# Rows of u of 1152 bytes instead of 1032, and buffers that begin at multiples of 128 bytes

## Chip, cores and metric

One Trainium2 chip; the kernel runs on one of its cores. The metric is the device time of one execution in microseconds (us), the median of several runs.

## What is computed

One decoder layer on 256 tokens of width 1024 in float32: a SwiGLU block (FFN), a mixer (a state-space branch and a retention branch side by side, gated and merged), a second FFN, and a last norm. Each of the three blocks reads `u`, the normed and modulated residual stream:

```python
u = modulate(rms_norm(h, norm_ffn1_w[l]), sh1, sc1)
h = h + FFN_RESIDUAL_WEIGHT * g1[:, None, :] * swiglu(u, ffn1_w_in[l], ffn1_w_out[l])
u = modulate(rms_norm(h, norm_mix_w[l]), sh2, sc2)
h = h + g2[:, None, :] * hybrid_mixer(u, positions, mix_w_in[l], ...)
u = modulate(rms_norm(h, norm_ffn2_w[l]), sh3, sc3)
h = h + FFN_RESIDUAL_WEIGHT * g3[:, None, :] * swiglu(u, ffn2_w_in[l], ffn2_w_out[l])
return rms_norm(h, norm_final_w)
```

In the FFNs `u` (256x1024) is multiplied by 1024x5632 and the result by 2816x1024; in the mixer `u` is multiplied by 1024x13344, and three smaller products follow.

## The kernel before

**Layout.** Features lie on the 128 partitions and tokens along the free dimension, so `u` is 8 rows (`kt`, 128 features each) of 256 tokens in every partition. Every large product is made of float32r matmuls in three terms: each operand is split into a high part and a remainder (`uh`/`ul`, `ah`/`al`, `wh`/`wl`), and `mm3` (lines 135 to 137) issues high·high, high·remainder and remainder·high into the same PSUM bank.

**Weights.** `load` brings 1 MB of weights into one of four stage buffers `wst` (8192 bytes per partition) through SyncE's DMA queue (line 111). `half` makes 512 KB of it into `wh` (a ScalarE copy, line 126) and `wl` (a VectorE subtraction, line 127), each of four buffers of 4096 bytes. TensorE then runs the matmuls of that half.

**Which operand moves.** A matmul has a stationary operand (loaded as weights of the array, 128 columns here) and a moving one, which streams through it (256, 258 or 512 columns here).
- `pair_project` and the first stage: weight halves stationary, a row of `uh` or `ul` moves, 256 columns. 48 matmuls for a 1 MB load.
- `early_project` runs the first four column blocks of a block on `u` that is not yet normed, with two more columns that hold the shift: 258 columns (`wide_at`). This is why a row of `u` has `T + 2` = 258 elements, 1032 bytes.
- `contract` and the branch steps (`bs`, `br`): weight halves stationary, rows of `ah`/`al` or of the mixer's slots (named `s`) move, 256 columns.
- `v_tile` (the `v` steps): slices of `u` stationary, weight halves move, 512 columns. The last contraction: `ah`/`al` stationary, weight halves move, 512 columns in its first block and 256 in the other two.

**The order of the work** is written out: loops in the FFNs, the table `ORDER` in the mixer. Each engine runs its instructions in that order and waits on semaphores. Other weights (for the modulation, `ada_w`) pass through the same stage buffers and are reduced on VectorE (line 179).

**Where a tile lies.** Pools stack their tiles one behind another in each partition, each at the next multiple of 32 bytes. In this program `wst`, `wh` and `wl` begin at 96 beyond a multiple of 128; `uh` too, `ul` at 32. A row of 1032 bytes moves the start by 8 bytes from row to row. The pools `fp` and `mx`, which hold `ah`, `al` and the slots, begin at a multiple of 128, with rows of 1024 bytes.

**The step scale of the state-space branch.** `dt_tile` computes a softplus on 64 columns in small tiles (`both`, `dtv`, ...). `decays` sends its result through DRAM (`rows`), and GpSimd's queue (POOL) loads it back as masks in buffers of the tag `m` (`wide`, five buffers) in the steps `ml.0` to `ml.3`.

Of the kernel before, what the change touches and what calls it, by code (L numbers as in the profile page):

```python
# [12 lines left out]
F32 = mybir.dt.float32  # L13
F32R = mybir.dt.float32r
# [4 lines left out]
P = 128  # L19
T = 256  # L20
D = 1024
KD = D // P
# [3 lines left out]
NH = 32  # L26
# [8 lines left out]
V_GB, V_SN, V_RN = 216, 232, 248  # L35
V_DS, V_DTB, V_AL = 264, 280, 312
N_VEC = 344

K_ID, K_TRI, K_M = 0, 128, 256
K_INV, K_SGN = 384, 385  # L40
# [37 lines left out]
def layer(ctx: ExitStack, tc: tile.TileContext, a, out, packing):  # L78
# [3 lines left out]
    cst = ctx.enter_context(tc.tile_pool(name="cst", bufs=1))  # L82
    wp = ctx.enter_context(tc.tile_pool(name="wp", bufs=1))
    sp = ctx.enter_context(tc.tile_pool(name="sp", bufs=1))
# [6 lines left out]
    def nm(s):  # L91
        uid[0] += 1
        return f"{s}_{uid[0]}"
# [36 lines left out]
    def split_into(hi, lo, src):  # L130
        act.copy(hi, src)
        dve.tensor_tensor(lo, src, hi.bitcast(F32), ALU.subtract)
# [17 lines left out]
    mean_m = k[:, K_M:K_M + P]  # L150
    ones = cst.tile([P, P], F32, name="ones")
    dve.memset(ones, 1.0)
    epsc = cst.tile([P, 1], F32, name="epsc")
    dve.memset(epsc, EPS)

    phase = {"load": None, "uses": []}
# [9 lines left out]
        with tc.issue_after(phase["load"]):  # L166
            phase["uses"].append(act.activation(*args, **kw).ins)

    col = cst.tile([P, N_VEC], F32, name="col")
    cb = cst.tile([P, D], F32, name="cb")  # L170
    raw = cst.tile([P, N_MOD, KD], F32, name="raw")
    modc = cst.tile([P, N_MOD, KD], F32, name="modc")
# [39 lines left out]
        return rs  # L212

    def new_u():
        full = [sp.tile([P, KD, T + 2], F32R, tag=n, name=nm(n), bufs=1) for n in ("uh", "ul")]
        return tuple(t[:, :, :T] for t in full) + tuple(full)

    def u_tile(u, f, t, jsh):
        sh = modc[:, jsh, f:f + 1]
        act.activation(u[0][:, f, :], t, AF.Identity, bias=sh)  # L220
        dve.scalar_tensor_tensor(u[1][:, f, :], t, sh, u[0][:, f, :].bitcast(F32),
                                 ALU.add, ALU.subtract)
# [20 lines left out]
    def modulated(ha, u, jsh, w, cols):  # L243
        rs = []
        ps = early_project(w, cols, u, 1, lambda: rs.append(rstd(sums, mean_m)))
        rs = rs[0]
        for f in range(KD):
            t = ha(f)
            dve.tensor_tensor(t, t, rs, ALU.mult)
            u_tile(u, f, t, jsh)  # L250
        b = sp.tile([P, 4], F32, tag="eb", name=nm("eb"), bufs=1)
        for i in range(4):
            dve.tensor_copy(b[:, i:i + 1], ps[i][:, T:T + 1])
            dve.tensor_tensor(ps[i][:, :T], ps[i][:, :T], rs, ALU.mult)
        return [(ps[i][:, :T], b[:, i:i + 1]) for i in range(4)]

    def early_project(w, cols, u, at_kt, between):
        sts = [load(w, 0, KD, c0, 256) for c0 in cols]
        ps = [proj_ps().rearrange("p f t -> p (f t)") for _ in range(2)]
        ps += [misc_ps() for _ in range(2)]  # L260
        for kh in range(2):
            hv = [half(st[:, 4 * kh:4 * kh + 4, :]) for st in sts]
            for kk in range(4):
                kt = 4 * kh + kk
                if kt == at_kt:
                    between()
                for i in range(2):
                    for f in range(2):
                        mm3(ps[2 * i + f][:, :T + 2], at(hv[i], al, kk, slice(f * P, (f + 1) * P)),
                            wide_at(u, kt), kt == 0, kt == KD - 1)  # L270
        return ps
# [63 lines left out]
    with tc.tile_pool(name="ep", bufs=1) as ep:  # L335
# [4 lines left out]
        for i in range(2):  # L340
            fetch(h[:, 4 * i:4 * i + 4, :].rearrange("p f t -> p (f t)"), "x",
                  lambda m, i=i: m[:, 512 * i:512 * i + 512].T.reshape(4, P, T).transpose(1, 0, 2))
# [133 lines left out]
    with tc.tile_pool(name="mx", bufs=1, reuse_waits="tile") as mx:  # L476
# [6 lines left out]
        def small(shape, tag, bufs=1):  # L483
            return mx.tile(shape, F32, tag=tag, name=nm(tag), bufs=bufs)

        def wide(shape, dt=F32):
            return mx.tile(shape, dt, tag="m", name=nm("m"), bufs=WIDE_BUFS)
# [2 lines left out]
        bT, cT = slot([P, 4, T]), slot([P, 4, T])  # L490

        dskip = col[:, V_DS:V_DS + 16]
        dtb, ahead = col[:, V_DTB:V_DTB + NH], small([P, NH], "ahead")
        rows = dp.tile([2, NH, P], F32, name="rows")

        def conv_pair(f0, dst):
# [17 lines left out]
        def need(t):  # L514
            if now[0] != t:
                now[0] = t
                table(table_of[t])
# [4 lines left out]
        def dt_tile():  # L522
            need("e")
            st = load(w_in, 0, KD, C_DT, NH)
            wd = wp.tile([P, 1024], F32R, tag="wh", name=nm("wh"), bufs=HALF_BUFS)
            wd = wd[:, :KD * 2 * NH].rearrange("p (k n) -> p k n", k=KD)
            split_into(wd[:, :, :NH], wd[:, :, NH:], st)
            ps = proj_ps()
            for kt in range(KD):
                uh, ul = at(u, al, kt)  # L530
                if kt:
                    pe.matmul(ps[:NH, 0, :], wd[:, kt, :NH], ul, start=False, stop=False)
                pe.matmul(ps[:2 * NH, 0, :], wd[:, kt, :], uh, start=kt == 0, stop=kt == KD - 1)
                if not kt:
                    pe.matmul(ps[:NH, 0, :], wd[:, kt, :NH], ul, start=False, stop=False)
            both = small([2 * NH, NH], "both")
            dve.tensor_tensor(both, ident[:2 * NH, :NH], ident[:2 * NH, NH:2 * NH], ALU.add)
            dtr = wide([2 * NH, T])
            act.copy(dtr, ps[:2 * NH, 0, :])
            ps = misc_ps()  # L540
            for c in range(2):
                pe.matmul(ps[:, c * NH:(c + 1) * NH], dtr[:, c * P:(c + 1) * P], both,
                          start=True, stop=True)
            v, e, s1, s2, pl = (small([P, 2, NH], n) for n in ("dtv", "dte_", "dts", "dts2", "dtp"))
            dve.tensor_tensor(v, ps[:, :64].rearrange("p (c h) -> p c h", c=2),
                              dtb.unsqueeze(1).broadcast_to([P] + x2), ALU.add)
            act.activation(e, v, AF.Abs)
            lookup(ahead, col[:, V_AL:V_AL + NH], AF.Exp)
            lookup(e, e, AF.Exp, scale=-1.0)
            dve.tensor_scalar(s1, e, 2.0, None, ALU.add)  # L550
            dve.reciprocal(s1, s1)
            dve.tensor_tensor(s1, s1, e, ALU.mult)
            dve.tensor_tensor(s2, s1, s1, ALU.mult)
            dve.tensor_scalar(pl, s2, 1.0 / 17, None, ALU.mult)
            for n in (15, 13, 11, 9, 7, 5, 3):
                dve.scalar_tensor_tensor(pl, pl, 1.0 / n, s2, ALU.add, ALU.mult)
            dve.scalar_tensor_tensor(pl, pl, 1.0, s1, ALU.add, ALU.mult)
            dve.tensor_scalar(v, v, 0.0, None, ALU.max)
            dve.scalar_tensor_tensor(dt, pl, 2.0, v, ALU.mult, ALU.add)
            dve.scalar_tensor_tensor(av, dt, -1.0, ahead.unsqueeze(1).broadcast_to([P] + x2),  # L560
                                     ALU.mult, ALU.mult)
# [310 lines left out]
        for q in range(2):  # L872
            for p2 in range(2):
                r = slice(2 * p2, 2 * p2 + 2)
                t = tot_r[q][:, r, :]
# [9 lines left out]
        def ha(f):  # L885
            return hA[f // 4][:, f % 4, :]
# [4 lines left out]
    with tc.tile_pool(name=nm("fp"), bufs=1, reuse_waits="tile") as fp:  # L891
# [43 lines left out]
        for bi, (c0, n) in enumerate(blocks):  # L935
# [15 lines left out]
            for tt in range(2):  # L951
                t = fp.tile([P, 512], F32, tag="t", name=nm("t"), bufs=2)[:, :n]
# [66 lines left out]
```

## Time and profile before

| | |
|---|---|
| median of 3 runs | 863.01 us (862.42 to 863.12) |
| the profiled execution | 864.84 us |
| its span, first to last instruction | 863.1 us |
| mean granted TensorE clock | 0.995 |
| PE busy | 847.8 us |
| DVE busy | 670.6 us |
| ACT busy | 509.2 us |
| HBM | 190.96 MB read, 223 GB/s over the span |

Matmuls overlap: one lasts about 0.28 us in the profile, but the next starts long before it ends. What a matmul costs is read from start to start, which is called its pace below. The profiled execution is 1.7 us longer than its span, and 1.8 us above the median of the runs without a profile.

### The profile page before, as it was taken

Reading aid. Unit: us, or ns where it says so; the run is one execution under the profiler, and the core shown is the slowest. Engines: PE = TensorE matmul, PEld = TensorE weight load, DVE = VectorE, ACT = ScalarE, POOL = GpSimd, SP = SyncE. Lnnn points to the kernel's source line nnn. Section 1 sums busy time; section 2 is a strip of 40 time slices with the busy share of each in tenths; the row PEclk is TensorE's granted clock in tenths of the full one; section 3 lists DMA queues with packets and bytes.
Section 4 is the critical chain, followed back from the end, with each engine's and each line's share of the span. In section 5 each row is a group of like instructions: output and inputs, shape, how many; then the busy total and the mean of one; then the engine's idle time right before and its main releaser. Section 6 shows DMA issues by size and latency. Waiting matters only on the chain.

```text
span 863.1 us, 16252 instructions
## 1 busy us (share of the span) xinstructions
PE 847.8 (98%) x6752; PEld 822.1 (95%) x6752; DVE 670.6 (78%) x1020; ACT 509.2 (59%) x722; POOL 10.3 (1%) x21
## 2 busy tenths in 40 slices
PE   6999999999999999999999999999999999999996
PEld 5999999999999989899999999999999999999896
DVE  6989798986989887688797778977979975455463
ACT  5355445455888687766464558765558644545342
POOL 0000000000110010000000000000000000000000
PEclk9999999999999999999999999999999999999998
DMA  9968878994595555445557664554554785454521
GB/s 350 414 247 323 312 272 311 359 355 161 189 319 194 191 185 177 177 147 196 196 196 293 222 221 156 211 205 156 218 213 180 260 317 189 154 185 176 189 87 49
DMA packets 30588, 193.09 MB, mean 224 GB/s; under 512 B 3489, under 2 KB 4001, under 8 KB 10802
## 3 DMA queue, kind: packets, MB, share of 16 engines
q1 hardware_dynamic: 28658, 186.34, 59.1%
q0 software_dynamic: 1568, 5.28, 1.9%
q8 instruction: 53, 0.87, 0.4%
q10 hardware_dynamic: 288, 0.44, 0.2%
q14 instruction: 21, 0.17, 0.1%
HBM read 190.96 MB, written 1.08 MB: 223 GB/s over the span
## 4 chain that ended last, share of the span: by engine, by line
PE 88%; issue 4%; DVE 3%; ACT 2%; DMA 2%; SPq 0%; DVEq 0%; ACTq 0%; POOLq 0%
PE proj L137 27%; PE proj L135 27%; PE proj L136 27%; PE misc L135 1%; PE misc L137 1%; PE misc L136 1%; DVE wl L127 1%; DMA ada<-in_ada_w_dram 1%; ACT wh L126 1%; DMA m<-rows 1%; PE misc L686 1%; PE misc L830 1%; PE misc L203 1%; DVE ada L179 0%; PE misc L696 0%
## 5 line engine op out<-in xcount | busy, mean ns | idle before, releaser
L126 ACT CAST wh<-wst 128x1024 fp32r<-128x1024 f32 (+3 forms) x281 | 289.6, 1034 | 265.9 <-PE proj L136 178.8
L127 DVE TENSOR_TENSOR wl<-wst,wh 128x1024 fp32r<-128x1024 f32 (+3 forms) x281 | 336.9, 1202 | 134.5 <-ACT wh L126 133.8
L135 PE MATMUL proj<-uh,wh 128*128 128x256 f32 (+1 forms) x1328 | 373.6, 282 | 2.3 <-ACT uh L220 2.3
L137 PE MATMUL proj<-uh,wl 128*128 128x256 f32 (+1 forms) x1328 | 374.7, 282 | 0.0
L136 PE MATMUL proj<-ul,wh 128*128 128x256 f32 (+1 forms) x1328 | 373.6, 282 | 0.0
L135 PEld LDWEIGHTS proj<-uh,wh 128*128 128x128 f32 x1328 | 250.1, 189 | 2.8 <-ACT uh L220 2.5
L136 PEld LDWEIGHTS proj<-ul,wh 128*128 128x128 f32 x1328 | 251.3, 189 | 0.3 <-issue 0.2
L137 PEld LDWEIGHTS proj<-uh,wl 128*128 128x128 f32 x1328 | 251.4, 189 | 0.2 <-issue 0.2
L135 PE MATMUL proj<-s,wh 128*128 128x256 f32 x320 | 89.9, 282 | 1.1 <-ACT s L752 0.8
L136 PE MATMUL proj<-s,wh 128*128 128x256 f32 x320 | 89.2, 279 | 0.0
L137 PE MATMUL proj<-s,wl 128*128 128x256 f32 x320 | 89.2, 279 | 0.0
L179 DVE SCALAR_TENSOR_TENSOR wst<-wst,cb 128x1024 f32<-128x1024 f32 x56 | 67.3, 1219 | 5.7 <-DMA wst<-in_ada_w_dram 5.6
L135 PEld LDWEIGHTS proj<-s,wh 128*128 128x128 f32 x320 | 60.0, 188 | 2.1 <-ACT s L752 1.7
L136 PEld LDWEIGHTS proj<-s,wh 128*128 128x128 f32 x320 | 60.2, 188 | 0.0
L137 PEld LDWEIGHTS proj<-s,wl 128*128 128x128 f32 x320 | 60.1, 188 | 0.0
L137 PE MATMUL proj<-ah,wl 128*128 128x256 f32 x176 | 49.1, 279 | 0.0
L135 PE MATMUL proj<-ah,wh 128*128 128x256 f32 x176 | 49.1, 279 | 0.0
L136 PE MATMUL proj<-al,wh 128*128 128x256 f32 x176 | 49.1, 279 | 0.0
L136 PE MATMUL proj<-wl,ah 128*128 128x256 f32 (+1 forms) x132 | 42.1, 319 | 0.0
L137 PE MATMUL proj<-wh,al 128*128 128x256 f32 (+1 forms) x132 | 42.1, 319 | 0.0
L135 PE MATMUL proj<-wh,ah 128*128 128x256 f32 (+1 forms) x132 | 42.1, 319 | 0.0
L159 ACT ACT_TABLE_LOAD x30 | 38.5, 1283 | 1.2 <-PEq L992 0.7
(234 smaller groups left out, 1069.0 us busy)
## 6 DMA issues: line engine op xcount, KB each, us to landing
wst<-in_mix_w_in_dram SPq DMA_DIRECT2D x52, 1024.0 KB, 4.9
wst<-in_ffn_w_in_dram SPq DMA_DIRECT2D x37, 1024.0 KB, 5.0
wst<-in_ada_w_dram SPq DMA_DIRECT2D x28, 1024.0 KB, 6.1
wst<-in_ffn_w_out_dram SPq DMA_DIRECT2D x17, 1024.0 KB, 4.9
ada<-in_ada_w_dram SPq DMA_DIRECT2D x16, 512.0 KB, 11.9
wst<-in_w_br_ssd_dram SPq DMA_DIRECT2D x8, 1024.0 KB, 4.9
wst<-in_w_br_ret_dram SPq DMA_DIRECT2D x8, 1024.0 KB, 5.2
wst<-in_ffn_w_in_dram SPq DMA_DIRECT2D x7, 896.0 KB, 12.6
```

Source lines behind the costliest of these rows:

```text
L126: act.copy(hi, v)
L127: dve.tensor_tensor(lo, v, hi.bitcast(F32), ALU.subtract)
L135: pe.matmul(o, l[0], r[0], start=first, stop=False, skip_group_check=skip)
L136: pe.matmul(o, l[0], r[1], start=False, stop=False, skip_group_check=skip)
L137: pe.matmul(o, l[1], r[0], start=False, stop=last, skip_group_check=skip)
L159: ins = act.preload_act_table_set(name).ins
L179: dve.scalar_tensor_tensor(st[:, i, :], st[:, i, :], 1.0, cb, ALU.mult, ALU.mult, accum_out=raw[:, j, f0 + i:f0 + i + 1])
L203: pe.matmul(ps[:, :T], mean, s, start=i == 0, stop=i == len(parts) - 1)
L686: pe.matmul(py[hh * 64:hh * 64 + 64, f * T + c * P:f * T + (c + 1) * P], xd[:, c, hl * 64:hl * 64 + 64], m[c][:, hl, :], start=True, stop= ...
L830: pe.matmul(py[:, eh, :], v[:, 0, es], sc[:, :T], start=True, stop=False)
```

## The change

A row of `u` gets 288 elements (1152 bytes, nine times 128), of which 256 or 258 are used as before. Small tiles ahead of the large ones (`epsc`, `col`) are padded so that the next large tile begins at a multiple of 128 bytes, and the tile `eb` behind them too. The small tiles of `dt_tile` become parts of one tile `work`, which takes a turn of the `m` buffers.

```diff
+LINE = 128
+U_ROW = T + LINE // 4
+PAD = 16
...
-    epsc = cst.tile([P, 1], F32, name="epsc")
+    epsc = cst.tile([P, LINE // 4], F32, name="epsc")[:, :1]
...
-    col = cst.tile([P, N_VEC], F32, name="col")
+    col = cst.tile([P, N_VEC + PAD], F32, name="col")[:, :N_VEC]
...
     def new_u():
-        full = [sp.tile([P, KD, T + 2], F32R, tag=n, name=nm(n), bufs=1) for n in ("uh", "ul")]
-        return tuple(t[:, :, :T] for t in full) + tuple(full)
+        full = [sp.tile([P, KD, U_ROW], F32R, tag=n, name=nm(n), bufs=1) for n in ("uh", "ul")]
+        return tuple(t[:, :, :T] for t in full) + tuple(t[:, :, :T + 2] for t in full)
...
-        b = sp.tile([P, 4], F32, tag="eb", name=nm("eb"), bufs=1)
+        b = sp.tile([P, LINE // 4], F32, tag="eb", name=nm("eb"), bufs=1)
...
-        dtb, ahead = col[:, V_DTB:V_DTB + NH], small([P, NH], "ahead")
+        dtb = col[:, V_DTB:V_DTB + NH]
...
-            both = small([2 * NH, NH], "both")
+            work = wide([P, 12, NH])
+            both, ahead = work[:2 * NH, 10], work[:, 11]
...
-            v, e, s1, s2, pl = (small([P, 2, NH], n) for n in ("dtv", "dte_", "dts", "dts2", "dtp"))
+            v, e, s1, s2, pl = (work[:, 2 * i:2 * i + 2] for i in range(5))
```

Where the tiles begin, in bytes from the start of a partition, as the pools place them (in brackets the remainder by 128):

| tile | before | after |
|---|---|---|
| `wst`, first of 4 | 26720 (96) | 26880 (0) |
| `wh`, first of 4 | 59488 (96) | 59648 (0) |
| `wl`, first of 4 | 75872 (96) | 76032 (0) |
| `uh`, row kt | 92256 + 1032 kt (96, 104, 112, 120, 0, 8, 16, 24) | 92416 + 1152 kt (0) |
| `ul`, row kt | 100512 + 1032 kt (32, 40, 48, 56, 64, 72, 80, 88) | 101632 + 1152 kt (0) |
| `ah`, row f | 117120 + 1024 f (0) | 119296 + 1024 f (0) |
| slots, 4096 bytes each | from 117120 (0) | from 119296 (0) |

No engine's instructions change their number, place or shape. What changes beside addresses is one wait, on GpSimd's queue. These are its rows of the steps `decays` (`rows<-m`) and `ml.0` and `ml.1` (two loads of `m` and two of `ec` each); in brackets the semaphores that a row waits for. Before:

```order
L624 DMA rows<-m_2669 32x2x128 [waits DVE_49]
L656 DMA m_2673<-rows 128x1024 [waits DMASW0_49]
L656 DMA m_2674<-rows 128x1024
L659 DMA ec_2672<-rows 64x4x128 x2
L656 DMA m_2680<-rows 128x1024
L656 DMA m_2681<-rows 128x1024 [waits PE_49,Activation_49]
L659 DMA ec_2679<-rows 64x4x128 x2
```

And now:

```order
L629 DMA rows<-m_2663 32x2x128 [waits DVE_49]
L661 DMA m_2667<-rows 128x1024 [waits DMASW0_49]
L661 DMA m_2668<-rows 128x1024
L664 DMA ec_2666<-rows 64x4x128 x2
L661 DMA m_2674<-rows 128x1024 [waits PE_49,Activation_49]
L661 DMA m_2675<-rows 128x1024 [waits Activation_49]
L664 DMA ec_2673<-rows 64x4x128 x2
```

Nothing moved. `work` takes one turn of the five `m` buffers, so that the first load of `ml.1` gets the buffer that `dtr` had (the wait for PE and ScalarE) and the second the one that `work` had (the added wait for ScalarE); before, the first got a fresh buffer.

## Rows read from the trace of the kernel before

**Rows 1.** The profile's page, its first line and the busy time of each engine (us, share of the span, instructions).

```profile
span 863.1 us, 16252 instructions
...
PE 847.8 (98%) x6752; PEld 822.1 (95%) x6752; DVE 670.6 (78%) x1020; ACT 509.2 (59%) x722; POOL 10.3 (1%) x21
```

**Rows 2.** Who TensorE (PE) waited for over the whole span: us in total, number of waits, the longest. These are the two largest of seven.

```profile
PE misc L360 <- DMA crow<-in_c_dram: 2.4, 1, 2.4
PE proj L135 <- ACT uh L220: 2.3, 1, 2.3
```

**Rows 3.** The page's chain of work that ended last, by engine, as shares of the span.

```profile
PE 88%; issue 4%; DVE 3%; ACT 2%; DMA 2%; SPq 0%; DVEq 0%; ACTq 0%; POOLq 0%
```

**Rows 4.** Timeline of PE, first and last matmul of an unbroken run in which u is the moving operand: 432 matmuls (nine pair projections of 48) in the mixer. Columns: start in us, duration in us, engine, line, operation, output<-inputs, array shape, shape of the moving operand.

```profile
456.58 0.28 PE L135 MATMUL proj<-uh,wh 128*128 128x256 f32 x1
...
507.82 0.28 PE L137 MATMUL proj<-uh,wl 128*128 128x256 f32 x1
```

**Rows 5.** The same, first and last matmul of two unbroken runs in which another tile moves: the 528 matmuls of the first FFN's contraction (`ah` and `al`), and 96 of two branch steps (the slots `s`).

```profile
146.05 0.28 PE L135 MATMUL proj<-ah,wh 128*128 128x256 f32 x1
...
207.54 0.28 PE L137 MATMUL proj<-ah,wl 128*128 128x256 f32 x1
...
422.54 0.28 PE L135 MATMUL proj<-s,wh 128*128 128x256 f32 x1
...
433.63 0.28 PE L137 MATMUL proj<-s,wl 128*128 128x256 f32 x1
```

**Rows 6.** The same for the last contraction, in which the weight halves move and `ah` and `al` are stationary: 132 matmuls of 512 columns, then 264 of 256 columns.

```profile
793.64 0.39 PE L135 MATMUL proj<-wh,ah 128*128 128x512 f32 x1
...
824.20 0.40 PE L137 MATMUL proj<-wh,al 128*128 128x512 f32 x1
824.43 0.28 PE L135 MATMUL proj<-wh,ah 128*128 128x256 f32 x1
...
855.56 0.27 PE L137 MATMUL proj<-wh,al 128*128 128x256 f32 x1
```

**Rows 7.** The same for one v step, in which the weight halves move and slices of u are stationary: 24 matmuls of 512 columns.

```profile
357.93 0.39 PE L135 MATMUL proj<-wh,uh 128*128 128x512 f32 x1
...
363.25 0.39 PE L137 MATMUL proj<-wh,ul 128*128 128x512 f32 x1
```

**Rows 8.** The same in the early projection ahead of the second FFN, 258 columns with u moving: the first and last of 49 matmuls.

```profile
670.07 0.28 PE L136 MATMUL misc<-ul,wh 128*128 128x258 f32 x1
...
675.82 0.28 PE L136 MATMUL misc<-ul,wh 128*128 128x258 f32 x1
```

**Rows 9.** Timeline of PE in the first microseconds of matmuls, two neighbours; then one stretch: us, busy us and instructions (x) of PE, PEld, DVE, ACT and POOL, the granted clock (a share of full speed), the DMA engines' share and GB/s.

```profile
20.71 0.41 PE L136 MATMUL proj<-ul,wh 128*128 128x256 f32 x1
20.92 0.41 PE L137 MATMUL proj<-uh,wl 128*128 128x256 f32 x1
...
19.40:22.00 2.60, 2.60 (x14) 2.60 (x14) 2.60 (x8) 1.73 (x3) 0.00 (x0) 0.50 1.01 411
```

**Rows 10.** Groups of PE instructions by line and shape (L135 alone; L136 and L137 have the same number each): count (x) | busy us, mean ns of one | idle us before.

```profile
L135 PE MATMUL proj<-uh,wh 128*128 128x256 f32 x1296 | 364.2, 282 | 2.3 <-ACT uh L220 2.3
L135 PE MATMUL proj<-s,wh 128*128 128x256 f32 x320 | 89.9, 282 | 1.1 <-ACT s L752 0.8 <-ACT s L131 0.2
...
L135 PE MATMUL proj<-ah,wh 128*128 128x256 f32 x176 | 49.1, 279 | 0.0
...
L135 PE MATMUL proj<-wh,uh 128*128 128x512 f32 x64 | 26.0, 406 | 0.0
...
L135 PE MATMUL proj<-wh,ah 128*128 128x256 f32 x88 | 24.7, 281 | 0.0
...
L135 PE MATMUL proj<-wh,ah 128*128 128x512 f32 x44 | 17.4, 395 | 0.0
...
L135 PE MATMUL misc<-uh,wh 128*128 128x256 f32 x48 | 13.2, 290 | 0.0
...
L135 PE MATMUL proj<-uh,wh 128*128 128x258 f32 x32 | 9.4, 294 | 0.0
```

**Rows 11.** Groups of ScalarE (ACT) and VectorE (DVE) instructions by line and shape, same columns.

```profile
L126 ACT CAST wh<-wst 128x1024 fp32r<-128x1024 f32 x255 | 267.1, 1049 | 248.5 <-PE proj L136 173.3 <-issue 37.4 <-PE proj L137 28.6
...
L131 ACT CAST s<-s 128x1024 fp32r<-128x1024 f32 x4 | 4.2, 1051 | 3.6 <-DVE s L728 3.6
...
L127 DVE TENSOR_TENSOR wl<-wst,wh 128x1024 fp32r<-128x1024 f32 x255 | 310.6, 1221 | 130.0 <-ACT wh L126 129.4 <-PE proj L136 0.2
...
L132 DVE TENSOR_TENSOR s<-s,s 128x1024 fp32r<-128x1024 f32 x4 | 4.9, 1226 | 0.0
```

**Rows 12.** The first stage: the timeline of the last `ul` row that is written there and of the first matmuls that read it.

```profile
54.07 0.48 DVE L221 SCALAR_TENSOR_TENSOR ul<-t,modc,uh 128x256 fp32r<-128x256 f32 x1
...
55.43 0.40 PE L135 MATMUL proj<-uh,wh 128*128 128x256 f32 x2
```

**Rows 13.** What SyncE's DMA queue waited for, the largest entry: us in total, times, the longest.

```profile
SPq L111 <- DVE wl L127: 525.3, 119, 12.2
```

**Rows 14.** One stretch behind the early projection (columns as in Rows 9).

```profile
670.00:680.00 10.00, 10.00 (x86) 10.00 (x86) 10.00 (x26) 8.65 (x14) 0.00 (x0) 1.00 0.47 174
```

**Rows 15.** Timeline of GpSimd's queue (POOL) at the two loads of `m` of the step `ml.1`.

```profile
237.57 1.12 POOL L656 DMA_DIRECT2D m<-rows  x2
```

## The prediction

> **What bounds the kernel now.** I read the busy times first: TensorE is busy for 847.8 of 863.1 us, VectorE for 670.6 and ScalarE for 509.2 [rows 1]. Since overlapping matmuls make a busy TensorE look full, I looked next at what it waits for: the two longest entries are 2.4 and 2.3 us, both before the kernel has got going [rows 2]. The chain that ended last is 88% TensorE [rows 3]. So the time is, almost everywhere, the number of matmuls times their pace, and what has to be found is whether the change alters the pace. An edit of addresses moves no instruction, so nothing else can give much.
>
> The pace is read from the first and the last matmul of unbroken runs, divided by their number less one:
> - u moves, 256 columns: (507.82 - 456.58) / 431 = 118.9 ns [rows 4].
> - `ah` and `al` move: (207.54 - 146.05) / 527 = 116.7 ns; slots move: (433.63 - 422.54) / 95 = 116.7 ns [rows 5].
> - weight halves move, `ah` stationary: (855.56 - 824.43) / 263 = 118.4 ns for 256 columns, (824.20 - 793.64) / 131 = 233.3 ns for 512 [rows 6].
> - weight halves move, u stationary: (363.25 - 357.93) / 23 = 231.3 ns for 512 [rows 7].
> - u moves, 258 columns: (675.82 - 670.07) / 48 = 119.8 ns [rows 8].
>
> The stages of these runs differ in what the other engines and the DMAs do, and the pace does not follow that: it goes with the tile that moves. [...]
>
> [...] The moving tiles at 116.7 ns begin every row at a multiple of 128 bytes; the weight halves begin at 96 beyond one and take 118.4; u's rows are spread over 16 starts and take 118.9 (the table of starts in the section on the change). From 256 to 512 columns with the same start the pace grows by 233.3 - 118.4 = 114.9 ns [rows 6]. What then remains per matmul, whatever its columns, is 1.8 ns for the slots, 3.5 for the weight halves and 4.0 for u. [...]
>
> **The change part by part.** All prices are per matmul and hold where TensorE is the bound.
> - *u moves, 256 columns.* By lines 135 to 137 there are 3 x (1296 + 48) = 4032 [rows 10]. 14 of them run at half clock [rows 9] and gain nothing. The rest come to the slots' pace: 4018 x (118.9 - 116.7) = 8.8 us.
> - *u moves, 258 columns.* 3 x (32 + 32) = 192 (`proj` and `misc`) [rows 10]. 116.7 x 258 / 256 = 117.6, so 192 x 2.2 = 0.4 us.
> - *Weight halves move in the last contraction.* 3 x 88 = 264 of 256 columns [rows 10] x (118.4 - 116.7) = 0.45 us. For the 132 of 512 columns no row has an aligned start; between nothing and twice 1.7 ns I take 1.7, the price per start, 0.2 us.
> - *Weight halves move in the v steps*, 192 matmuls [rows 10]: between nothing and 192 x 1.7 = 0.3 us. They run at 231.3 ns already, 2 ns below the last contraction's 233.3, so I take nothing.
> - *Weight halves as stationary operand*, 3 x (1296 + 48 + 64 + 320 + 176) = 5712 matmuls. From above: u moving with weights at 96 takes 118.9, weights moving with `ah` at 0 takes 118.4; if all of that difference were the stationary start, 5712 x 0.5 = 2.9 us. From below: with u stationary, off every boundary, 512 columns take 231.3, with `ah` on one 233.3; if that were the stationary start, it would cost 5712 x 2.0 = 11.4 us. The two contradict each other, and the loading itself lies under the matmul before. I take nothing and keep both ends.
> - *ScalarE and VectorE.* A 128x1024 copy takes 1049 ns between tiles at 96 and 1051 between slots; the subtraction 1221 and 1226 [rows 11]. Nothing.
> - *The tile `work` and its wait on GpSimd's queue.* The second mask load of `ml.1` now waits for ScalarE's use of `work`. That precedes `av`, on which `decays` and with it the first load of `ml.0` depend, so it is over when the queue comes there; the loads stand at 237.57 us [rows 15]. Behind it are two loads of `ec`, not needed until the second group of heads. Nothing.
> - *What may take gain back.* In the first stage VectorE writes the last row of `ul` until 54.07 + 0.48 = 54.55 us, and TensorE reads it from 55.43 [rows 12]. TensorE comes there 7 x 42 x 2.2 ns = 0.65 us sooner, which leaves 0.23 us: kept. Behind the second early projection VectorE is busy for 10.00 of 10 us [rows 14]; matmuls there can't all come sooner, and I take off 0.2 us, what 86 of them would gain. The weight transfers are early: SyncE's queue waits 525.3 us in all for a stage buffer to come free [rows 13]. The 7.3 us behind the last matmul stay.
>
> [...]
>
> Sum: 8.8 + 0.4 + 0.45 + 0.2 - 0.2 = 9.65 us. The profiled execution took 864.84 us, so 855.2 by that; the runs without a profile are 1.8 us below, so 863.0 - 9.65 = **853.4 us**.
>
> **The rivals.**
> - *The stationary start counts too*, as the upper bound above: 853.4 - 2.9 = 850.5 us. For it: the half nanosecond between the runs. Against: u's rows also begin at finer offsets than the weights, which explains it as well.
> [...]
> - *Another engine becomes the bound* in the stretches with u, and half of the gain goes: 858.2 us. For it: VectorE's full stretch [rows 14]. Against: its 670.6 us over the span.
> - *It is not the start but the spacing of 1024 bytes*, which `ah` and the slots have and u's rows have neither before (1032) nor after (1152). Then u falls to 118.4 at most, 4018 x 0.5 = 2.0 us plus 0.65 of the last contraction: 860.4 us. Against: the weight halves of the last contraction have rows of 1024 bytes too in their 256-column blocks, and are slow.
> - *The change does not reach the pace at all*: 863 us.
> - *Slower: aligned stationary weights cost*, as the lower bound: from 1.7 ns per matmul (9.65 / 5712) it outweighs the gain, and at 2.0 gives 853.4 + 11.4 = 864.8 us. Against: slots move at 116.7 past weights at 96 and `ah` exactly as fast, and the 118.4 of the last contraction, with stationary tiles on the boundary, is below u's 118.9.
>
> **How the numbers follow.** A measurement of this kernel can tell about 0.2% (1.7 us) from no change. Chances: the forecast (851.5 to 855.5) 0.70; stationary too 0.07; the large gain 0.02; half lost 0.07; spacing 0.05; no change 0.04; slower 0.05. Those below 861.3 make faster 0.91, the rest 0.04 and 0.05. The range from 849.5 to 858.5 us takes in the forecast, the stationary case and the half; it leaves out 0.16.
>
> **What would show it.** The run of [rows 4] comes to 116.7 ns, that is 50.3 us instead of 51.24; the two of [rows 5] keep theirs; the 264 of the last contraction take 30.7 us instead of 31.13; no longer waits in TensorE's list. The forecast is wrong if u's runs stay above 118, if the runs of [rows 5], whose moving tiles stay aligned and whose weights now are too, change their pace by more than 0.3 ns, or if TensorE's waits grow by more than 2 us.

## The result and the profile after

The changed kernel takes **867.08 us** (median of 6 runs, 866.48 to 868.48), the kernel before 863.12 in the same comparison: 1.004 times as long, 95% interval 1.0026 to 1.0053. The forecast was 853.4 us. The change makes the kernel slower by 0.4%, and the whole of the expected gain is missing too. Two executions of kernels below are in no ratio, 1180.31 us with the weights at 192 (mean granted clock 0.656) and 2935.89 us with the slots at 128.

The page after, as [rows 1] and [rows 3]: its first line, the busy times, and the chain that ended last.

```profile
span 865.7 us, 16252 instructions
...
PE 852.0 (98%) x6752; PEld 827.2 (96%) x6752; DVE 671.8 (78%) x1020; ACT 509.3 (59%) x722; POOL 10.3 (1%) x21
...
PE 91%; issue 4%; ACT 2%; DVE 1%; DMA 1%; DVEq 0%; ACTq 0%; POOLq 0%
```

TensorE is busy for 4.2 us more with the same 6752 matmuls; VectorE and ScalarE are where they were. Nor has TensorE found a new wait: the two longest entries of its list are those of [rows 2].

```profile
PE misc L364 <- DMA crow<-in_c_dram: 2.5, 1, 2.5
PE proj L139 <- ACT uh L224: 2.3, 1, 2.3
```

So the pace has changed. These are the first and the last matmuls of the unbroken runs after that answer to [rows 4] to [rows 8] (432 with u, 528 with `ah`, 96 with slots, the last contraction's 132 and 264, one v step's 24, and 49 of 258 columns).

```profile
458.69 0.28 PE L139 MATMUL proj<-uh,wh 128*128 128x256 f32 x1
...
509.94 0.28 PE L141 MATMUL proj<-uh,wl 128*128 128x256 f32 x1
...
145.25 0.28 PE L139 MATMUL proj<-ah,wh 128*128 128x256 f32 x1
...
208.48 0.28 PE L141 MATMUL proj<-ah,wl 128*128 128x256 f32 x1
...
424.02 0.28 PE L139 MATMUL proj<-s,wh 128*128 128x256 f32 x1
...
435.41 0.28 PE L141 MATMUL proj<-s,wl 128*128 128x256 f32 x1
...
796.96 0.39 PE L139 MATMUL proj<-wh,ah 128*128 128x512 f32 x1
...
826.65 0.39 PE L141 MATMUL proj<-wh,al 128*128 128x512 f32 x1
826.88 0.28 PE L139 MATMUL proj<-wh,ah 128*128 128x256 f32 x1
...
858.43 0.28 PE L141 MATMUL proj<-wh,al 128*128 128x256 f32 x1
...
359.06 0.40 PE L139 MATMUL proj<-wh,uh 128*128 128x512 f32 x1
...
364.40 0.40 PE L141 MATMUL proj<-wh,ul 128*128 128x512 f32 x1
...
673.42 0.28 PE L140 MATMUL misc<-ul,wh 128*128 128x258 f32 x1
...
679.22 0.28 PE L140 MATMUL misc<-ul,wh 128*128 128x258 f32 x1
```

| what moves, columns | matmuls in all | pace before, ns | pace after, ns | change, us |
|---|---|---|---|---|
| u, 256 | 4032 | 118.9 | (509.94 - 458.69) / 431 = 118.9 | 0 |
| u, 258 | 192 | 119.8 | 5.80 / 48 = 120.8 | +0.2 |
| `ah`, `al`, 256 | 528 | 116.7 | 63.23 / 527 = 120.0 | +1.7 |
| slots, 256 | 960 | 116.7 | 11.39 / 95 = 119.9 | +3.1 |
| weight halves in the last contraction, 256 | 264 | 118.4 | 31.55 / 263 = 120.0 | +0.4 |
| weight halves in the last contraction, 512 | 132 | 233.3 | 29.69 / 131 = 226.6 | -0.9 |
| weight halves in the v steps, 512 | 192 | 231.3 | 5.34 / 23 = 232.2 | +0.2 |

The sum is 4.7 us, against 4.2 more busy time of TensorE and 4.0 between the medians. u, which was to give 8.8 us, gave nothing. `ah`, `al` and the slots lay at a multiple of 128 bytes before and after, and yet they lost 3.3 ns per matmul. Modulo 128, what changed for them is only where the weight halves begin; modulo 256 their own start moved too, from 128 to 0.

### The profile page after: what moved, and what is told of

It reads as the page before. It is cut to its first block, busy times and chain, and to the rows that moved or that the text cites. A ratio compares the mean times of both kernels' runs of the same rounds, so it can differ in the third digit from the quotient of the medians.

```text
span 865.7 us, 16252 instructions
## 1 busy us (share of the span) xinstructions
PE 852.0 (98%) x6752; PEld 827.2 (96%) x6752; DVE 671.8 (78%) x1020; ACT 509.3 (59%) x722; POOL 10.3 (1%) x21
## 4 chain that ended last, share of the span: by engine, by line
PE 91%; issue 4%; ACT 2%; DVE 1%; DMA 1%; DVEq 0%; ACTq 0%; POOLq 0%
PE proj L140 28%; PE proj L139 28%; PE proj L141 28%; PE misc L139 1%; PE misc L141 1%; PE misc L140 1%; DMA m<-rows 1%; PE misc L691 1%; PE misc L207 1%; PE misc L835 1%; ACT L163 0%; ACT wh L130 0%; PE misc L364 0%; PE misc L701 0%; ACT s L171 0%
## 5 line engine op out<-in xcount | busy, mean ns | idle before, releaser
L139 PE MATMUL proj<-s,wh 128*128 128x256 f32 x320 | 90.9, 285 | 0.9 <-ACT s L757 0.8
L140 PE MATMUL proj<-s,wh 128*128 128x256 f32 x320 | 90.4, 283 | 0.0
L139 PEld LDWEIGHTS proj<-s,wh 128*128 128x128 f32 x320 | 61.2, 192 | 2.0 <-ACT s L757 1.6
L140 PEld LDWEIGHTS proj<-s,wh 128*128 128x128 f32 x320 | 61.3, 192 | 0.0
```

What stands on the lines that cost most here:

```text
L139: pe.matmul(o, l[0], r[0], start=first, stop=False, skip_group_check=skip)
L140: pe.matmul(o, l[0], r[1], start=False, stop=False, skip_group_check=skip)
```

## The experiments

After the result four theories stood against each other. **Pair**: the pace depends on where the moving and the stationary operand begin, both together, and equal starts are bad. **Moving alone**: what counts is the moving operand's start, with a period other than 128 (slots and `ah` begin at 128 beyond a multiple of 256 before and at one after). **Stationary alone**: aligned weight halves are bad by themselves. **One spot**: some absolute address was met by chance. In the names below a start is given modulo 128 or 256 bytes, and "64 with 0" means a moving start of 64 and a stationary start of 0; the weight halves are `wh` and `wl`.

**A sweep of starts.** TensorE alone, in groups of 72 matmuls (36 with 512 columns) with the three terms' pattern; the rest of the layer is left out.

```diff
+        hi = tiles["mh"][:, (a + p * r) // 4:(a + p * r) // 4 + n]
+        lo = tiles["ml"][:, (a2 + p * r) // 4:(a2 + p * r) // 4 + n]
+        wh = tiles["wh"][:, b // 4 + s * 128:b // 4 + s * 128 + 128]
+        wl = tiles["wl"][:, b // 4 + s * 128:b // 4 + s * 128 + 128]
+        pe.matmul(ps[:, :n], wh, hi, start=i == 0, stop=False)
+        pe.matmul(ps[:, :n], wh, lo, start=False, stop=False)
+        pe.matmul(ps[:, :n], wl, hi, start=False, stop=i == kts - 1)
```

> The layer is left out: the kernel loads x, copies it into two moving tiles and two stationary tiles, and runs only matmuls of mm3's pattern in groups. A group is named by the start of the moving rows (a), the step from row to row (p) and the start of the stationary slices (b), in bytes beyond a multiple of 1024; 72 matmuls of 256 columns, or 36 of 512. No other engine and no DMA works beside them. Theory 1 (pair): the pace is set by both starts together, as the two operands are read side by side. It expects about 116.7 ns at moving 0 with stationary 96, 120.0 at 0 with 0, 118.4 at 96 with 0, and 118.9 for the row step 1032 with 96, as the layer shows. Theory 2 (moving alone, by 256): slots and ah lay 128 beyond a multiple of 256 before and on one after, and that is what made them slower; it expects 116.7 for a128 and 120 for a0 and a256 at every b. Theory 3 (stationary alone): 120 for every a at b0, b128 and b256, and 116.7 for every a at b96.

First and last matmul of the group with the moving tiles and the weights both at 64, rows of 1024 bytes:

```profile
205.13 0.28 PE L61 MATMUL a64p1024b64x<-mh,wh 128*128 128x256 f32 x1
...
213.65 0.28 PE L63 MATMUL a64p1024b64x<-mh,wl 128*128 128x256 f32 x1
```

8.52 / 71 = 120.0 ns, or 119.9 from the starts in whole nanoseconds, which the table uses. Read in this way (0 with 0, the disturbed first group, from the third sweep below), the paces in ns are:

| weights at | moving at 0 | 32 | 64 | 96 | 128 |
|---|---|---|---|---|---|
| 0 | 119.9 | 116.8 | 113.4 | 120.0 | 118.7 |
| 32 | 118.3 | 119.8 | 117.9 | 117.9 | 119.9 |
| 64 | 117.8 | 118.3 | 119.9 | 117.9 | 117.9 |
| 96 | 117.4 | 117.8 | 118.3 | 119.9 | 117.9 |
| 128 | 118.6 | 118.7 | 113.5 | 118.2 | 119.9 |

The diagonal stands out: equal starts take 119.8 or 119.9 ns at all five places; off it, 96 with 0 and 128 with 32 are as slow. Neither a row nor a column is constant, so neither operand sets the pace alone. One absolute spot is not it either: 64 with 128 has the pace of 64 with 0, and in the later sweeps 192 with 0 and 0 with 64 come to it too (113.5 to 113.7). The pair theory's own values were met only in part: 0 with 96 took 117.4 (116.7 expected) and 96 with 0 took 120.0 (118.4 expected). With 512 columns equal starts are the better ones, 226.8 and 227.6 ns (96 with 96, 0 with 0) against 228.8 to 234.3, as in the last contraction after.

**The weights' move taken back, and the weights' move alone.** Two kernels from either side.

```diff
 # after, weight halves at 96 again ("w96")
-    epsc = cst.tile([P, LINE // 4], F32, name="epsc")[:, :1]
+    epsc = cst.tile([P, 1], F32, name="epsc")
-    col = cst.tile([P, N_VEC + PAD], F32, name="col")[:, :N_VEC]
+    col = cst.tile([P, N_VEC], F32, name="col")
     def new_u():
+        sp.tile([P, 40], F32, name="upad")
 # before, weight halves at 0, all else at its old remainder ("w0")
-    epsc = cst.tile([P, 1], F32, name="epsc")
+    epsc = cst.tile([P, LINE // 4], F32, name="epsc")[:, :1]
-    col = cst.tile([P, N_VEC], F32, name="col")
+    col = cst.tile([P, N_VEC + PAD], F32, name="col")[:, :N_VEC]
     def new_u():
+        sp.tile([P, 24], F32, name="upad")
```

> The changed kernel with the stage and the weight halves back at 96 beyond a multiple of 128 (the paddings of epsc and col taken out, 160 bytes put ahead of u); u, activations and slots stay exactly where the change puts them. Theory 1 (pair): slots and ah go from 120.0 to 116.7 ns, 1488 matmuls, 4.9 us; u's rows, all on a multiple of 128 with weights at 96, too, 118.8 to 116.7 over 4018, 8.4 us; the last contraction back to 118.4 and 233.3; about 854 us. Theory 2 (moving alone): nothing changes, 867 us. Theory 3 (stationary alone): as theory 1 here.

> The kernel before with only the stage and the weight halves moved to multiples of 128 (epsc and col padded, 96 bytes put ahead of u, so that u, activations and slots keep their remainders by 256). Theory 1 (pair): slots and ah go from 116.7 to 120.0 ns, 1488 matmuls, 4.9 us more; u is open, its rows have 16 different starts against the weights either way, so about 118.9; near 868 us. Theory 2 (moving alone, by 256): slots and ah stay at 116.7 and u at 118.9, 863 us. Theory 3 (stationary alone): everything gets 3.3 ns slower, 863 + 5500 x 3.3 ns = 881 us.

With the weights' move taken back the ratio to before is 0.9985 (0.9975 to 0.9995), 862.8 us; with the weights' move alone it is 1.0035 (1.0023 to 1.0047), 867.14 us. **Moving the weight halves, without touching u, makes a slowdown of the same size**, with intervals that overlap. Its parts differ: `ah` and the slots take 118.7 there, not 120, and the 512 columns of the last contraction stay at 233.3. Slots with the weights' move alone, in the run of [rows 5]:

```profile
423.85 0.28 PE L138 MATMUL proj<-s,wh 128*128 128x256 f32 x1
...
435.12 0.28 PE L140 MATMUL proj<-s,wl 128*128 128x256 f32 x1
```

11.27 / 95 = 118.6 ns instead of 116.7, though the slots begin at 128 beyond a multiple of 256 as before; the sweep has 118.7 for that pair. With the weights' move taken back:

```profile
454.08 0.28 PE L139 MATMUL proj<-uh,wh 128*128 128x256 f32 x1
...
504.84 0.28 PE L141 MATMUL proj<-uh,wl 128*128 128x256 f32 x1
```

u comes to 50.76 / 431 = 117.8 ns. That is what u's own rows can be worth: 1.1 ns, half of the forecast's 2.2. This kernel still fell 9 us short of what the pair theory had forecast for it (about 854). Half of that is u, which stayed 1.1 ns above the forecast's 116.7 (4018 x 1.1 = 4.4 us); and slots took 120.0 in some runs and 117.4 in others.

**The slots' period.** after, but `ah` and slots at 128 beyond a multiple of 256, where they lay before.

```diff
-    epsc = cst.tile([P, LINE // 4], F32, name="epsc")[:, :1]
+    epsf = cst.tile([P, LINE // 4], F32, name="epsc")
+    epsc = epsf[:, :1]
...
-        b = sp.tile([P, LINE // 4], F32, tag="eb", name=nm("eb"), bufs=1)
+        b = epsf[:, 4:8]
```

> The changed kernel with slots, ah and al 128 bytes lower, so that they begin 128 beyond a multiple of 256 as before the change (the tile eb goes into unused columns of epsc); weights and u stay on their multiples. Theory 1 (pair, by 128): slots and ah stay at 120.0 ns, 867 us. Theory 2 (moving alone, by 256): they go back to 116.7, 1488 x 3.3 ns = 4.9 us less, 862 us. Theory 3: 120.0, 867 us.

866.55 us, ratio 1.0027 (1.0017 to 1.0037); slots and `ah` at 118.7, the very pace of the weights' move alone. The moving tile's period is not the cause: that theory wanted 116.7 ns and 862 us. But the 128 bytes did change the pace (119.9 before them), so two starts 128 bytes apart are not alike, although the pair theory took them to be; 256 bytes apart they are (119.7 for 256 with 0 in the sweep). The run of 432 with u in this kernel:

```profile
457.14 0.28 PE L139 MATMUL proj<-uh,wh 128*128 128x256 f32 x1
...
507.91 0.28 PE L141 MATMUL proj<-uh,wl 128*128 128x256 f32 x1
```

50.77 / 431 = 117.8 ns, where the changed kernel has 118.9, with u and the weights at the same starts as there. The changed kernel itself holds one run of 96 with u, at 330 us, at 117.9, and the first sweep has 117.8 to 117.9 for rows of 1152 with the weights at 0, 64, 96 and 128. So rows of 1152 can run at either pace, and the weights at 0 do not forbid the faster one.

**u alone at 64, and all moving tiles at 64**, the weight halves staying at 0. A pad of 64 bytes ahead of u; for u alone `eb` gets 64 bytes less.

```diff
     def new_u():
+        sp.tile([P, 16], F32, name="upad")
```

> The changed kernel with 64 bytes ahead of u and 64 fewer behind it: u alone begins 64 past a multiple of 128, weights, slots, ah and al lie as the change has them. Theory 1 (pair): u 118.8 to 113.3 ns over 4018 matmuls, up to 22 us less, 845 us; slots and ah stay at 120.0. Rival: as for the kernel with all of them moved, above 860 us.

> The changed kernel with one pad of 64 bytes ahead of u: weights stay on multiples of 128, u, ah, al and the slots begin 64 past one. Theory 1 (pair): slots and ah 120.0 to 113.3 ns over 1488 matmuls, 9.9 us; u 118.8 to 113.3 over 4018, 22 us, if the row step of 1152 keeps the distance, less if rows at 0 and 128 by 256 differ; the last contraction 0.3 us slower; 867 - 32 = 835 us, and at least 857 from the slots alone. Rival (the pace that the sweep shows without other engines does not carry over, or another engine takes over as the bound): above 860 us, with TensorE's waits grown by the gain.

u alone: 861.47 us, 0.9972 (0.9962 to 0.9983), u at 117.8, slots and `ah` still at 120.0. All: **859.6 us, 0.9944 (0.9924 to 0.9964)**, slots at 117.8, the last contraction's 256 columns at 113.4. Leaving the boundary gains 0.56% on the kernel before, about 4.8 us, half of what the change was to gain by coming onto it. The pair theory's forecasts of 845 and 835 us were missed by 16 and 25 us: u came to 117.8 and not to 113.3, as the rival (above 860 us) had it for u alone; for all moved 859.6 lies just below that bound.

**u's rows alone.** 1152 bytes, the paddings undone: weights and u at 96, `ah` and slots at 128.

> The kernel after with its three paddings undone: rows of u stay 1152 bytes, but weight halves and u's first rows begin at 96 beyond a multiple of 128 (equal starts again, and ul too), the slots and ah at a multiple of 128 as in the kernel before. If the pair of starts sets the pace, this is for u the case of the kernel after moved by 96 bytes, u 118.8 ns, while slots and ah return to the 116.7 of the kernel before; the time is that of the kernel before, 863 (862 to 865). If a multiple of 128 bytes matters in itself for the moving operand, as the prediction had it, u stays at 118.4 or above although all its rows begin at the same offset, and gains nothing either; that rival differs only if u comes below 118.0, which would say that uniform rows alone are the gain: 4018 x 1 or more, 859 or below.

864.47 us, 1.0011 (1.0001 to 1.0021). u stays at 118.9 although every row now begins alike modulo 128 (modulo 256 rows of 1152 bytes alternate between two starts). `ah` came to 117.8 and the slots to 117.8 in some runs and 116.8 in others, not to 116.7 throughout: 528 x 1.1 + 960 x 0.5 = 1.1 us, most of what lies between 864.5 and the 863 expected. These tiles and the weights begin, modulo 256, exactly where they do in the kernel before, so the pair of starts does not fix the pace by itself.

**All moving tiles at 32.** As with 64, a pad of 32 bytes.

> The kernel after with a pad of 32 bytes ahead of u: u, ah, al and the slots begin at 32 beyond a multiple of 128, the weight halves at 0. The distance from weights to slots is that of the kernel before (32 bytes), with nothing on the prediction's good side: all moving tiles are off the boundary. If the distance of the two starts decides, slots and ah return from 120.0 to between 116.7 and 118.4 and u falls below 118.4: 858 to 863 us. If the moving tile's own start decides, as the prediction had it, u, ah and slots all pay 1.7 ns or more on top of the slots' 116.7: at least 118.4, 867 us or more.

860.16 us, 0.9961 (0.9948 to 0.9973): slots at 116.7, the pace that [rows 5] had at the same distance of 32 with the slots on a boundary. The prediction's rule, by which nothing here is aligned and all is slow (867 or more), falls.

**The stationary operand moved instead.** after, with the weight halves 64 bytes earlier; the tiles from `epsc` to the stage move along, u and all behind it stay.

```diff
-    epsc = cst.tile([P, LINE // 4], F32, name="epsc")[:, :1]
+    epsc = cst.tile([P, LINE // 8], F32, name="epsc")[:, :1]
...
     def new_u():
+        sp.tile([P, 16], F32, name="upad")
```

> The kernel after with its weight halves 64 bytes earlier and nothing else moved: u, ah and slots stay at 0, the weight halves lie at 192 beyond a multiple of 256. Every distance between a moving and a stationary start is that of the kernel with all moving tiles at 64, but it is the other operand that has left the boundary. If the distance decides, its paces come back: slots 117.4, ah 115.6, u 117.4, the last contraction's 256 columns 113.1, 859.6 us (858 to 861). If the moving operand's own start decides, these keep the 120.0 of the kernel after, 867 us; if off-boundary weights are bad by themselves, 867 or more.

```profile
419.26 0.28 PE L139 MATMUL proj<-s,wh 128*128 128x256 f32 x1
...
430.45 0.28 PE L141 MATMUL proj<-s,wl 128*128 128x256 f32 x1
...
453.42 0.28 PE L139 MATMUL proj<-uh,wh 128*128 128x256 f32 x1
...
504.18 0.28 PE L141 MATMUL proj<-uh,wl 128*128 128x256 f32 x1
...
819.54 0.28 PE L139 MATMUL proj<-wh,ah 128*128 128x256 f32 x1
...
849.36 0.28 PE L141 MATMUL proj<-wh,al 128*128 128x256 f32 x1
```

Slots 11.19 / 95 = 117.8, u 50.76 / 431 = 117.8, the last contraction 29.82 / 263 = 113.4: the paces of the kernel with all moving tiles at 64, and 858.57 us, 0.9935 (0.9923 to 0.9948). Since u, `ah` and the slots stayed where the changed kernel has them, on their boundary, this is the plainest proof that the weights' start counts: 64 bytes in its place are worth about 1%. Only `ah` (117.8) did not come to the expected 115.6, which was the mean of two paces (below).

**Does the pair fix the pace?** Two more sweeps (the layer left out) asked for other starts, other widths, and the same pair behind different predecessors.

> As the first sweep, without the layer; a name now gives the start of the high moving rows (a), of the remainder's moving rows (l), the row step (p), the stationary start (b) and the columns (n). In the first sweep moving rows at 64 past a multiple of 128 with stationary slices on one ran at 113.3 ns, equal starts at 120.0, the rest between 116.7 and 120.7. [...] Theory 4 (chance of one spot: the 113.3 belongs to the absolute place 64): a192, a320, a576 or b256 leave it.

> No layer is computed, only TensorE groups of a moving start a and a stationary start b (bytes beyond a multiple of 1024), rows of 1024 bytes. First part, 128 columns with b from 0 to 96: if the 111.67 ns of the sweep before are the loading of the stationary operand, and a start of that operand costs something in the loading, the pace must change with b; if it stays within 0.3 ns for all twelve pairs, the loading has a fixed price and what the starts cost arises where a matmul is longer than its loading. Second part, the same starts several times, 256 columns, b = 0: if the pace belongs to the pair of starts alone, all nine groups of a64b0 agree (113.3 or 117.8) and so do the four of a32b0 and three of a0b0 (118.3, 120.0); if it depends on what ran before, a64b0 shows both 113.3 and 117.8. Third part, b = 96, 64 and 32: equal starts (a64b64, a32b32) again 120.0.

It does not fix it alone. In the second sweep 64 with 0 took 117.8 where the first had 113.4, and of the pairs for which the pair theory expected 113.3 again only 192 with 0 came near it (113.6); 320 or 576 with 0 and 64 with 128, 256 or 512 took 117.8. Two groups of the third sweep, 48 matmuls each of the same pair, the first behind a group of start 56, the other behind one of start 0:

```profile
107.79 0.28 PE L57 MATMUL g16a64b0n256x<-mh,wh 128*128 128x256 f32 x1
...
113.12 0.28 PE L59 MATMUL g16a64b0n256x<-mh,wl 128*128 128x256 f32 x1
...
130.04 0.28 PE L57 MATMUL g20a64b0n256x<-mh,wh 128*128 128x256 f32 x1
...
135.58 0.28 PE L59 MATMUL g20a64b0n256x<-mh,wl 128*128 128x256 f32 x1
```

5.33 / 47 = 113.4 and 5.54 / 47 = 117.9 ns: one pair, two steady paces. The stretch of the first (columns as in [rows 9]; ACT and POOL stand behind PEld, since VectorE has no work here) shows no other engine, the full clock and no DMA:

```profile
106.00:114.00 8.00, 8.00 (x72) 8.00 (x71) 0.00 (x0) 0.00 (x0) 1.00 0.00 0
```

So neither of these chose. 64 with 0 shows 113.4 twice and 117.8 or 117.9 five times there. The start of the group before does not choose either: behind 32 the pair took 117.9 once and 113.4 once in this sweep, and behind 56 it took 113.4 here and 117.8 in the second sweep. Nor does the PSUM buffer, of which the groups take eight in turn: the fast group above shares its buffer with a group of 64 with 0 at 117.8. 0 with 0 shows 119.6 to 119.9 each time, and so do 32 with 32 and 64 with 64. So equal starts showed one pace, the slow one, and other pairs have a choice whose rule these runs do not give.

The layer shows the choice at work. In the kernel with all moving tiles at 64, the 528 matmuls of the first contraction have the pair 64 with 0 throughout:

```profile
142.25 0.28 PE L139 MATMUL proj<-ah,wh 128*128 128x256 f32 x1
...
173.47 0.28 PE L140 MATMUL proj<-al,wh 128*128 128x256 f32 x1
173.65 0.39 PE L141 MATMUL proj<-ah,wl 128*128 128x256 f32 x1
173.87 0.28 PE L139 MATMUL proj<-ah,wh 128*128 128x256 f32 x1
...
179.08 0.28 PE L140 MATMUL proj<-al,wh 128*128 128x256 f32 x1
180.00 0.38 PE L141 MATMUL proj<-ah,wl 128*128 128x256 f32 x1 [0.64 <-DVE wl L131]
```

The first 266 run at 31.22 / 265 = 117.8 ns. Then two starts come 0.18 and 0.22 us after the one before, and from there on the pace is 5.21 / 46 = 113.3 ns, also behind the wait for `wl` at 180.00. With the weights at 192 the same contraction has no such break and stays at 117.8. So the pace changed where the stream of matmuls was interrupted; that an interruption is what sets it was not tested.

The widths settle another point. 48 matmuls of 128 columns, weights at 16:

```profile
37.20 0.27 PE L57 MATMUL g3a0b16n128x<-mh,wh 128*128 128x128 f32 x1
...
42.45 0.28 PE L59 MATMUL g3a0b16n128x<-mh,wl 128*128 128x128 f32 x1
```

5.25 / 47 = 111.7 ns. The ten groups of 128 columns that were not at the sweep's disturbed start show 111.6 to 111.7, whatever the two starts; 192 columns take 112.1, hardly more. Half the columns, and only 8 ns less than 256: in these groups there is a floor per matmul that the columns do not set. What stays the same in them is the load of 128 stationary columns; whether the load makes the floor is not shown, as no group with a smaller load was run. Beyond it, 320 and 384 columns take 146.7 and 173.4 ns, 26.7 more for 64 columns, so 0.417 ns for each.

**Slots at 192.** All at 64 as above, `ah` and slots 128 bytes earlier (the diff of "The slots' period").

> The kernel with all moving tiles at 64 (weight halves at 0, u, ah and slots at 64 beyond a multiple of 256), but ah and the slots 128 bytes earlier, so at 192 beyond a multiple of 256; u and the weight halves stay. In the sweep without history, the moving start 192 took 113.33 ns in all five of its groups, while 64 took 113.33 in two and 117.8 in six. If the pair of starts decides (modulo 256), ah and slots come to 113.3 here: 959 x 4.1 + 529 x 2.3 = 5.1 us below the kernel with all at 64, 854.5 us. If two steady paces are open to each such pair and what runs before chooses, they stay between 115 and 118 and the time between 857 and 861. If only the distance modulo 128 counts, nothing changes at all: 859.6.

**857.57 us, 0.9924 (0.9909 to 0.994): the lowest time of the study, faster than both kernels**, though its interval overlaps that of the weights at 192. Two of its slot runs, 96 matmuls each, with the same tiles' starts:

```profile
420.29 0.28 PE L139 MATMUL proj<-s,wh 128*128 128x256 f32 x1
...
431.06 0.28 PE L141 MATMUL proj<-s,wl 128*128 128x256 f32 x1
...
442.71 0.28 PE L139 MATMUL proj<-s,wh 128*128 128x256 f32 x1
...
453.90 0.28 PE L141 MATMUL proj<-s,wl 128*128 128x256 f32 x1
```

10.77 / 95 = 113.4 and 11.19 / 95 = 117.8: the two paces of the sweep, in the layer, within one execution. `ah` stays at 117.8. The theory that 192 always gives 113.3 (854.5 us) falls; the choice between two paces is what remains, and the time lies where that expectation put it (857 to 861).

All kernels of the layer side by side, starts modulo 256, paces in ns (u in the run of 432, `ah` in the run of 528, slots in the run of 96 near 420 us, last contraction with 256 columns):

| kernel | weights | u | slots, `ah` | u pace | `ah` pace | slots pace | last | ratio to before |
|---|---|---|---|---|---|---|---|---|
| before | 96 | spread | 128 | 118.9 | 116.7 | 116.7 | 118.4 | 1 |
| after | 0 | 0, 128 | 0 | 118.9 | 120.0 | 119.9 | 120.0 | 1.0040 |
| weights' move alone | 0 | spread | 128 | 119.0 | 118.7 | 118.6 | 118.7 | 1.0035 |
| its move taken back | 96 | 0, 128 | 0 | 117.8 | 117.3 | 120.0 | 120.0 | 0.9985 |
| slots at 128 | 0 | 0, 128 | 128 | 117.8 | 118.7 | 118.7 | 120.0 | 1.0027 |
| u's rows alone | 96 | 96, 224 | 128 | 118.9 | 117.8 | 117.8 | 118.4 | 1.0011 |
| u at 64 | 0 | 64, 192 | 0 | 117.8 | 120.0 | 119.8 | 120.0 | 0.9972 |
| all at 32 | 0 | 32, 160 | 32 | 117.8 | 116.7 | 116.7 | 118.3 | 0.9961 |
| all at 64 | 0 | 64, 192 | 64 | 117.8 | 117.8, then 113.3 | 117.8 | 113.4 | 0.9944 |
| weights at 192 | 192 | 0, 128 | 0 | 117.8 | 117.8 | 117.8 | 113.4 | 0.9935 |
| slots at 192 | 0 | 64, 192 | 192 | 117.8 | 117.8 | 113.4 | 117.8 | 0.9924 |

In the profiled execution of "all at 32" the run of `ah` also held 2.3 us in which TensorE stood still; its pace is the mean without these.

## Why the prediction was wrong

- *What bounds the kernel* was right: the number of matmuls times their pace. What moved, in every kernel above, is the pace, but for short stalls in two of them (all at 32, all at 64).
- *The step that failed* is the reading of the 2.2 ns between u (118.9) and the slots (116.7): they were put down to the start of the moving tile alone. The four runs that carried it differed in two things, where the moving and where the stationary tile begins, and only one was looked at. Slots and weights lay 32 bytes apart, modulo 128, and at that distance 116.7 is one of the possible paces, on a boundary or off it (all at 32: 116.7; u's rows alone: 117.8). Bringing all starts to one remainder made distance 0 of it, and the fast operand fell to 120.0. The remainder itself was misread too: the 114.9 ns from 256 to 512 columns changes with the starts. With equal starts it is 226.6 - 120.0 = 106.6 ns, and 13.4 ns remain. The term of 8.8 us came out as 0: uniform rows brought u to 117.8 in other kernels, half of what was forecast, and here nearly all of u stayed at 118.9. What was to keep its pace lost 4.8.
- *The stationary operand at nothing* rested on "The two contradict each other, and the loading itself lies under the matmul before". The contradiction (aligning it gains up to 2.9 us by one comparison and costs up to 11.4 by the other) was the trace's sign that a quantity was missing, namely the other operand; it was taken for a sign that there was nothing. The loading does lie there in the profile: before, the load for u's matmul at 457.18 us takes 0.19 us from 457.06, and the matmul before it 0.28 us from 457.06. That it therefore costs nothing was the author's estimate, and no run shows it.
- *The last contraction* went both ways: 256 columns lost 1.6 ns where 1.7 were to be gained, 512 gained 6.7 where 1.7 were: a price per start, as it was taken for them, no run shows. *v steps* nothing forecast, 0.2 us lost. *u, 258 columns* lost 0.2 us where 0.4 were to be gained. *What may take gain back* was not put to the test, since there was no gain.
- *ScalarE and VectorE*, *`work`* and *no new waits* were right. The copy takes 1049 ns as in [rows 11], the subtraction 1223 instead of 1221; the second loads of [rows 15] are issued at 238.50 us, 0.9 us later, as everything behind the first contraction.
- *The rivals.* "Slower: aligned stationary weights cost" had the sign, but less than half of the size (864.8 is 1.8 us above the kernel before, 4.0 were measured), and its place is another: not 2.0 ns on each of 5712 matmuls, whatever they meet, but 3.3 ns on the 1488 that had a better distance before. It had a chance of 0.05. The large gain, at 0.02, did not come: no pace of 256 columns came below 113.3 ns. "Spacing" is not the cause either: rows of 1152 take 117.8 or 118.9, and rows of 1024 lie anywhere between 113.4 and 122.1.
- The tests that the prediction set fell as it had said a wrong forecast would show: u stayed above 118, and the runs of [rows 5] moved by 3.2 and 3.3 ns.

Here the two operands are not independent in what they cost: 64 bytes in the weights' place alone moved the last contraction from 120.0 to 113.4 ns and the slots from 119.9 to 117.8. Where that arises no run shows.

**What stays open.** That the two starts act together is shown. Why, is not; that the starts are equal is not the whole rule either, since 96 with 0 and 128 with 32 are as slow (120.0 and 119.9), and 0 with 96 took 117.4 in the first sweep and 120.0 in some slot runs of the layer. Nor is it known what picks one of the steady paces for a pair; neither the start of the group before nor the PSUM buffer does it alone.

## What to carry to other kernels

Here, where each matmul brings its own stationary tile, the pace went with both operands' starts (113.3 to 122.1 ns for 256 columns): compare runs by the pair, and with 256 columns try one of the two tiles moved off the other (a pad of 64 bytes; here the slots came from 119.9 to 117.8 ns by it) before trusting any single "aligned" address. With 512 columns the equal starts were the better ones (226.6 to 227.6 ns against 228.8 to 234.3). When two comparisons bound the same term with opposite signs, a second variable is at work; vary it before giving the term a nothing. Such a pad costs one line, and here the choice of it was worth 1.2%, from 1.0040 to 0.9924.

## What was not expected of the hardware

- 256 columns took anything from 113.3 to 122.1 ns per matmul, with the same work and other starts or another order (granted clock 1.000 in the sweeps, 0.995 after). The slowest were moving tiles at 8 bytes beyond a multiple of 128 (120.0 to 122.1 in the first sweep).
- Equal starts, with rows of 1024 or 2048 bytes, were among the slow ones for 256 columns (119.6 to 120.0) and the best for 512 (226.6 to 227.6).
- One pair of starts can hold either of two paces (113.4 or 117.8) over a whole run of 96 matmuls and more, in one execution, and can change from one to the other within a run.
- In the sweeps a matmul with its own 128-column load took 111.6 to 111.7 ns at 128 columns and 112.1 at 192.
